# A two-layer trunk on one core: the attention's gate is summed in the first FFN, VectorE scales all columns of the handing over, and its first weight is split sooner

## The chip, the cores and the metric

The kernel runs on one core of a Trainium2 chip. The metric is the device time of one execution, in microseconds. Every kernel is also run once with the hardware profiler; that execution has its own time, and the times in the profile are counted from the start of its span.

## The reference

One sequence of 256 tokens with 2048 columns goes through two layers. Layer 0 is a causal pooling mixer and a SwiGLU FFN; then one latent key/value set is computed; layer 1 is latent attention over that set and a second FFN. Every sub-layer has its shift, scale and gate, which come from one vector `c`:

```python
sc = jax.nn.silu(c)
for i in range(DEPTH):                      # 2
    shift_m, scale_m, gate_m, shift_f, scale_f, gate_f = jnp.split(sc @ mod_w[i] + mod_b[i], N_MOD, axis=-1)
    if i == N_A:                            # layer 1: shared latent keys and values
        kv_shift, kv_scale = jnp.split(sc @ kv_mod_w + kv_mod_b, 2, axis=-1)
        h_kv = modulate(rmsnorm(x, kv_in_norm), kv_shift, kv_scale)
        kv = shared_kv(h_kv, w_dkv, kv_norm, w_uk, w_uv, w_kr, cos, sin)
    h = modulate(rmsnorm(x, norm_mix[i]), shift_m, scale_m)
    y = pool_mixer(h, pool_w[i], pool_scale[i]) if i < N_A else mla_mixer(h, kv, ...)
    x = x + gate_m[:, None, :] * y
    h = modulate(rmsnorm(x, norm_ffn[i]), shift_f, scale_f)
    x = x + gate_f[:, None, :] * swiglu(h, ffn_gate[i], ffn_up[i], ffn_down[i])
return rmsnorm(x, final_norm)
```

The FFN's inner width is 5632; there are 16 heads. All data are fp32.

## The kernel before

**Products.** Each fp32 weight tile of 1 MB (`raw`, 128 x 2048) is loaded by SyncE's queue (SP), and split into an upper half (ACT, L374) and a lower half (VectorE or DVE, L376), both `hl` tiles. The activations have two halves as well (`act` tiles), and a product is three: upper by upper, upper weight by lower activation, lower weight by upper activation (L398). A weight makes 24 products of 128x128 by 128x512 on TensorE (PE); the last third of them needs the lower weight. For the last weight of a sum the products go token block by token block (there are two, `tok` 0 and 1), so the lower weight is needed after 8 products there.

**The background.** The modulation vectors are products of one row with big matrices, and PE doesn't make them (but for the first ones): `Part.unit` loads one tile of 1 MB (L210) and sums it on DVE, one instruction over 128 x 2048 (L211, with a short reading of the accumulator). 168 such units stand in one list. Each split of a weight calls `tick()`, which adds `rate` to a credit and starts a unit when it reaches one; `plan(left, units)` first does what the plan before left over, and then sets the rate such that `left` units remain after so many ticks. `hold()` stops the units, `release(left, units)` goes on at a new rate. The loads share a ring of six `raw` tiles with the weights, and SP's queue issues both in program order. When all 16 units of a gate are summed, `spread` (L291 to L297) turns it on PE, copies it on ACT, writes it to DRAM from ACT's queue and broadcasts it into the one `gate` tile from GpSimd's (POOL).

**The stages**, by the profile: 0 to 190 us the pooling mixer; then the first FFN. It begins six of eleven chunks block by block as blocks of its input become ready (`start_ffn`, to about 389); in its last block round `todo` units are issued with the weights. `FFN_STEPS` then mixes projections (p), transpositions (t) and down projections (d); the last down projection (d3, 856 to 889) handles four column blocks (j = 0 to 3) of two weights each. Its results are gated and added (`piece`, L611 and L612); parts that are known before are added ahead (`known`, L604 and L605).

**The handing over** (889 to 917): the fourth column block's products aren't run by `ffn` but by `then_attention`, which is written out in the order in which each engine is to work (`manual_schedule`; elsewhere a scheduler sets it). It mixes the old products (`h.old`, L407) with the first products of the latent keys and values (a for the first weight, b for the second, 0 and 1 for the token block; each is three lists of four: [0] upper by upper, [1] lower weight, [2] lower activation). Between them stand the norm (L470, L472), the scaling of columns by it (`scale`, L476: DVE for column block 0, POOL for block 1), the transposition on PE (`turn`, L482), the shift and scale (`upper` on ACT, L490; `whole` on ACT, L499, or on DVE, L497) and the lower half (`lower`, DVE, L503). `split_upper` (ACT, L517) and `split_lower` (DVE, L520) split the two weights.

**After that** come the rest of the latent keys and values (to 936), the keys and values of the heads and the query latent (to 1012), the heads (to 1098: scores L1383 to L1386, softmax L1388 to L1401, transposition L1407, weights split in smaller pieces at L1362 and L1363), the output projection (to 1163), a second handing over with one column block, and the second FFN.

## Time and profile before

| | |
|---|---|
| median of 3 runs | 1918.96 us (1916.93 to 1919.68) |
| the profiled execution | 1918.19 us |
| its span | 1916.4 us |
| mean granted clock of TensorE | 0.987 |
| busy, share of the span: PE, DVE, ACT, POOL | 97%, 73%, 44%, 1% |
| background sums (L211): count, mean | 168, 2284 ns |
| lower splits (L376): count, mean | 289, 2289 ns |
| upper splits (L374): count, mean | 289, 1918 ns |
| DMA, mean over the span | 300 GB/s |

In rows of the profile, `L376 DVE TENSOR_TENSOR hl<-raw,hl 128x2048` is line 376 of the kernel, engine, operation, what it writes and reads, and its size. In the order of time a row has the start, the duration from the first to the last of `x` instructions in a row, and in brackets the idle time before it with what ended it. A row of windows has the window, its length and then for PE, PE's weight loads, DVE, ACT and POOL the busy time and the number of instructions, then the granted clock, the DMA engines' share and GB/s.

### The profile page before, as it was taken

How to read it: one execution, taken by the hardware profiler on the slowest of the kernel's cores; microseconds unless marked ns; L12 is line 12 of the kernel's file. 1: busy time of each engine (PE TensorE's matmuls, PEld its weight loads, DVE VectorE, ACT ScalarE, POOL GpSimd, SP SyncE). 2: the span in 40 equal slices, each digit the busy share in tenths (PEclk: the TensorE clock that was granted, in tenths of full speed). 3: DMA queues.
4: the chain of work that ended last, by engine and by line, in shares of the span. 5: the costliest groups of instructions: out<-in, count | busy, mean ns of one | idle time of the engine just before them, and what ended most of it. 6: DMA issues, size and time to landing. Idle time of an engine off the chain costs nothing.

```text
span 1916.4 us, 21930 instructions
## 1 busy us (share of the span) xinstructions
PE 1862.8 (97%) x8813; PEld 1507.8 (79%) x8813; DVE 1402.7 (73%) x1391; ACT 850.2 (44%) x958; POOL 26.9 (1%) x32
## 2 busy tenths in 40 slices
PE   7689999999999999999999999999999999999998
PEld 3255888888888888887889888888888888888887
DVE  2148799999788777799899966889785556645556
ACT  3125643444433334244678745634444433343343
POOL 0000000000000000002100000000000000000000
PEclk9789999999999999999999999999999999999999
DMA  9999998879998888897597775988776666665651
GB/s 399 398 418 417 368 364 333 319 299 361 357 344 332 327 330 326 332 373 274 212 371 291 293 278 194 397 318 335 260 284 240 241 240 239 249 222 205 220 198 44
DMA packets 86647, 574.98 MB, mean 300 GB/s; under 512 B 10977, under 2 KB 15505, under 8 KB 18321
## 3 DMA queue, kind: packets, MB, share of 16 engines
q1 hardware_dynamic: 86018, 570.42, 77.8%
q0 software_dynamic: 432, 3.15, 0.4%
q8 instruction: 69, 1.13, 0.2%
q14 instruction: 32, 0.26, 0.0%
q10 hardware_dynamic: 96, 0.02, 0.0%
HBM read 567.24 MB, written 6.32 MB: 299 GB/s over the span
## 4 chain that ended last, share of the span: by engine, by line
PE 69%; issue 22%; DMA 3%; DVE 3%; ACT 1%; SPq 0%; POOL 0%; POOLq 0%; DVEq 0%; ACTq 0%
PE ps L398 58%; DMA raw<-in_mod_w_dram 3%; PE ps L256 2%; PE ps L973 2%; PE ps L407 2%; PE ps L1288 2%; DVE raw L211 1%; PE ps L729 1%; PE ps L1197 1%; PE ps L540 0%; DMA raw<-in_mod_block_dram 0%; PE ps L196 0%; PE ps L948 0%; PE ps L770 0%; DVE hl L376 0%
## 5 line engine op out<-in xcount | busy, mean ns | idle before, releaser
L398 PE MATMUL ps<-hl,act 128*128 128x512 f32 x6744 | 1539.5, 390 | 1.9 <-DVE hl L376 1.0
L398 PEld LDWEIGHTS ps<-hl,act 128*128 128x128 f32 x6744 | 1263.0, 188 | 264.7 <-DVE hl L376 1.8
L376 DVE TENSOR_TENSOR hl<-raw,hl 128x2048 fp32r<-128x2048 f32 x289 | 661.1, 2289 | 253.2 <-ACT hl L374 252.5
L374 ACT ACTIVATE hl<-raw 128x2048 fp32r<-128x2048 f32 x289 | 553.1, 1918 | 647.8 <-PE ps L398 572.1
L211 DVE SCALAR_TENSOR_TENSOR raw<-raw,s_row 128x2048 f32<-128x2048 f32 x168 | 383.2, 2284 | 3.6 <-DMA raw<-in_mod_wt_dram 3.6
L256 PE MATMUL ps<-raw,s_strip 128*32 128x512 f32 x392 | 65.2, 760 | 34.6 <-DMA raw<-in_mod_w_dram 33.5
L698 DVE TENSOR_TENSOR act<-ps,act 128x512 f32<-128x512 f32 x96 | 64.5, 685 | 17.5 <-PE ps L398 17.5
L256 PEld LDWEIGHTS ps<-raw,s_strip 128*32 128x32 f32 x392 | 9.5, 121 | 70.0 <-DMA raw<-in_mod_w_dram 46.3
L784 DVE TENSOR_TENSOR x<-ps,x 128x512 f32<-128x512 f32 x32 | 22.1, 690 | 38.8 <-PE ps L398 38.8
L1288 PE MATMUL ps<-act,hl 128*128 128x256 f32 x384 | 49.6, 287 | 0.0
L1288 PEld LDWEIGHTS ps<-act,hl 128*128 128x128 f32 x384 | 48.3, 195 | 0.7 <-DVE act L1253 0.2
L407 PE MATMUL ps<-hl,act 128*128 128x512 f32 x192 | 47.0, 400 | 1.2 <-DVE act L503 1.2
L732 ACT ACTIVATE act<-ps 128x512 fp32r<-128x512 f32 x44 | 23.6, 594 | 50.0 <-PE ps L729 37.6
L407 PEld LDWEIGHTS ps<-hl,act 128*128 128x128 f32 x192 | 35.2, 188 | 10.7 <-ACT act L490 2.3
L263 DVE COPY t2k<-ps 128x256 f32<-128x256 f32 x4 | 1.7, 425 | 52.9 <-ACT t2k L262 52.9
L427 ACT ACTIVATE junk<-x 128x512 bf16<-128x512 f32 x23 | 14.5, 629 | 53.2 <-DVE x L612 37.6
L802 DVE TENSOR_TENSOR t2k<-ps,t2k 128x512 f32<-128x512 f32 x24 | 16.5, 689 | 28.5 <-PE ps L398 28.5
L798 ACT ACTIVATE t2k<-ps 128x512 f32<-128x512 f32 x24 | 14.2, 590 | 47.9 <-PE ps L398 47.9
L973 PEld LDWEIGHTS ps<-act,act 128*128 128x128 f32 x128 | 24.7, 200 | 11.6 <-issue 8.4
L696 ACT ACTIVATE act<-ps 128x512 f32<-128x512 f32 x32 | 19.1, 597 | 29.0 <-PE ps L398 28.8
L973 PE MATMUL ps<-act,act 128*128 128x256 f32 x128 | 31.9, 402 | 0.0
L733 DVE TENSOR_TENSOR act<-ps,act 128x512 fp32r<-128x512 f32 x44 | 28.1, 683 | 0.9 <-ACT act L732 0.9
(222 smaller groups left out, 911.6 us busy)
## 6 DMA issues: line engine op xcount, KB each, us to landing
raw<-in_mod_wt_dram SPq DMA_DIRECT2D x136, 1024.0 KB, 5.8
raw<-in_ffn_gate_dram SPq DMA_DIRECT2D x88, 1024.0 KB, 5.8
raw<-in_ffn_up_dram SPq DMA_DIRECT2D x88, 1024.0 KB, 5.1
raw<-in_ffn_down_dram SPq DMA_DIRECT2D x88, 1024.0 KB, 5.2
raw<-in_mod_w_dram SPq DMA_DIRECT2D x48, 1024.0 KB, 12.1
raw<-in_kv_mod_wt_dram SPq DMA_DIRECT2D x32, 1024.0 KB, 7.1
raw<-in_w_o_dram SPq DMA_DIRECT2D x16, 1024.0 KB, 6.1
raw<-in_mod_block_dram SPq DMA_DIRECT2D x8, 1024.0 KB, 12.5
```

Of the source, the lines that this page charges most:

```text
L211: dve.scalar_tensor_tensor(out=r, in0=r, scalar=1.0, in1=s_row, op0=ALU.mult, op1=ALU.mult, accum_out=self.sums[:, self.n:self.n + 1])
L256: pe.matmul(self.bank[m * STRIP:(m + 1) * STRIP, :], lhsT=weights(k), rhs=r[:, k, i, :], start=first, stop=last)
L374: hi_ins = act.activation(hi, r, AF.Copy)
L376: lo_ins = dve.tensor_tensor(out=lo, in0=r, in1=hi.bitcast(F32), op=ALU.subtract)
L398: pe.matmul(banks[tok], lhsT=t_[:, i, k, tok * P:(tok + 1) * P], rhs=w[:, k, :], start=first and n < len(part), stop=last and n >= len(ord ...
L407: pe.matmul(bank, lhsT=t_[:, i, k, tok * P:(tok + 1) * P], rhs=w[:, k, :], start=first and n == 0, stop=last and n == len(order) - 1)
L698: dve.tensor_tensor(out=part, in0=banks[tok], in1=part, op=ALU.add)
L732: act.activation(m[:, 0, :, ts_], v, AF.Copy)
L733: dve.tensor_tensor(out=m[:, 1, :, ts_], in0=v, in1=m[:, 0, :, ts_].bitcast(F32), op=ALU.subtract)
L784: dve.tensor_tensor(out=x[:, tok, js], in0=banks[tok], in1=x[:, tok, js], op=ALU.add)
L973: pe.matmul(mixed[g][:, n % 2, :], lhsT=wp[g][:, k, ns], rhs=pool_all[g // 2][:, g % 2, k, :], start=k == 0, stop=k == KL - 1)
L1288: pe.matmul(pt[:, h, :], lhsT=w(h0 + h, k), rhs=t_[:, i, k, :], start=n == 0, stop=n == 3 * KL - 1)
```

## The change

There are seven edits.

1. The plan of the background. The 16 units of the attention's gate (`n_mix`) no longer count among those that are left after the first FFN; `FFN0_UNITS` is 94 for 95, and `plan` and `hold`/`release` beside the query latent and the heads go. The first FFN after `start_ffn` now takes 89 units for 74 (91 in 94 ticks for 75 in 95), the keys and values 7 for 6, query latent and heads none for 19, the output projection 8 for 5. The second FFN keeps its 40. The gate's transposition and broadcast move from the heads into the keys and values.
2. `scale` runs on DVE for every column block; before, POOL did block 1.
3. In the last down projection `hold()` stands at column block 2, not 3.
4. `split_lower(w[0])` in the handing over stands ahead of the old products.
5. In `start_ffn`, block round 0, the eight units go with the third to the tenth of the twelve begun weights, not with the first eight. (In the first FFN the upper split of the second weight thereby comes to stand, on ACT, between the two halves of the four L1044, and three of that weight's products after the first four of the first weight's on PE.)
6. `run(a1[2], b0[2], ...)` for `run(b0[2], a1[2], ...)`.
7. `HEAD_UNITS` and `WO_LATE` have no use any more and go; `WO_UNITS` is 9 for 8.

```diff
--- before.py
+++ after.py
@@ -61,12 +61,11 @@
 BEGUN = 6
 ASIDE = 5
 
-FFN0_UNITS, MLA_UNITS, HEAD_UNITS, WO_UNITS, FFN1_UNITS = 95, 4, 16, 8, 60
+FFN0_UNITS, MLA_UNITS, WO_UNITS, FFN1_UNITS = 94, 4, 9, 60
 
 KNOWN = (1, 3, 5, 7, 9, 10, 11, 12)
 
-
-LATE, MLA_LATE, WO_LATE = 3, 5, 3
+LATE, MLA_LATE = 3, 5
 
 V_C, V_NM, V_NF, V_KVIN, V_KVN, V_QN, V_PS, V_B, V_KB, V_END = 0, 16, 48, 80, 96, 100, 104, 120, 312, 344
 
@@ -473,8 +472,8 @@
 
         def scale(self, tok, j):
             self.turned[tok, j] = t2k([P, CH]), ps_t().rearrange("p (k t) -> p k t", k=KL), t2k([P, KL, P])
-            (dve if j == 0 else pool).tensor_scalar(out=self.turned[tok, j][0], in0=x[:, tok, j * CH:(j + 1) * CH],
-                                                    scalar1=self.rstd[:, tok:tok + 1], scalar2=None, op0=ALU.mult)
+            dve.tensor_scalar(out=self.turned[tok, j][0], in0=x[:, tok, j * CH:(j + 1) * CH],
+                              scalar1=self.rstd[:, tok:tok + 1], scalar2=None, op0=ALU.mult)
 
         def turn(self, tok, j):
             xr, pt, _ = self.turned[tok, j]
@@ -745,7 +744,7 @@
             for j in range(ND):
                 js = slice(j * CH, (j + 1) * CH)
                 banks = [ps_t() for _ in range(NT)]
-                if last and j == ND - 1:
+                if last and j == ND - 2:
                     hold()
                 if last and j == ND - 1:
                     weights = [w_unit(wd[c, j]) for c in g]
@@ -884,7 +883,7 @@
                         begun[c][which].block(j, hT[j])
                     if n == 2 * len(begun) - 5:
                         pieces = ahead(j + 1)
-                    if todo:
+                    if todo and (j > 0 or n + 2 >= 2 * len(begun) - todo):
                         pump(1)
                         todo -= 1
                 pump(todo)
@@ -1107,9 +1106,9 @@
     for j in range(ND):
         sf_block(1, j, C_SF1, C_AF1)
     mod_part(1, 5, gate_to, "ffn1")
-    n_ffn1, n_blocks, n_mix = KD, KD // 2, KD
+    n_ffn1, n_blocks = KD, KD // 2
     n_late = n_ffn1 + LATE * n_blocks
-    n_all = n_ffn1 + ND * n_blocks + n_mix
+    n_all = n_ffn1 + ND * n_blocks
 
     hT, begun = start_ffn(0, first, hidden_T, lambda j, parts: halves_T(j, parts), ND - 1)
     plan(n_all + MLA_LATE, FFN0_UNITS)
@@ -1127,6 +1126,7 @@
         hkv, rstd = h.hT, h.rstd
         w = [w_load_of(dkv(j)) for j in range(2)]
         split_upper(w[0])
+        split_lower(w[0])
         run(h.old(0))
         h.start()
         h.piece(0)
@@ -1134,7 +1134,6 @@
         split_upper(w[1])
         h.scale(0, 0)
         h.scale(0, 1)
-        split_lower(w[0])
         fs = h.old(1)
         run(fs[:-KL])
         h.turn(0, 0)
@@ -1163,7 +1162,7 @@
         h.lower(0, 1)
         h.turn(1, 1)
         h.upper(1, 1)
-        run(b0[2], a1[2], b1[0], b1[1])
+        run(a1[2], b0[2], b1[0], b1[1])
         h.whole(1, 1, dve)
         h.lower(1, 1)
         run(b1[2])
@@ -1315,7 +1314,6 @@
     pool.memset(krT, 0.0)
     rope_end(kr_t, [(slice(0, ROPE), krT[0:ROPE, 0, :]), (slice(ROPE, P), krT[ROPE:P, 1, :])])
 
-    plan(n_all - n_mix - WO_LATE, HEAD_UNITS)
     cq = [ps_t() for _ in range(NT)]
     for j in range(ND):
         if len(hmx) < ND:
@@ -1430,11 +1428,9 @@
     pairs = H // HG
 
     act.activation(small([P, 1]), ones[:, 0:1], AF.Exp)
-    hold()
     heads = [project_heads(g) for g in range(2)]
     for o in heads:
         o.finish()
-    release(n_all - n_mix - WO_LATE, HEAD_UNITS - 8)
 
     w_o, ob = a["w_o"], []
```

In the changed kernel line numbers are one lower up to the keys and values, and two lower from the heads on.

How the instructions move on DVE, at three places. First the first FFN's last down projection, before: from the last transposition's lower half (L733) to the lower split of the second weight of column block 1 (`hl_5636`); L611 and L612 add results, L604 and L605 what is known.

```order
484 L733 TENSOR_TENSOR act_5487<-ps_5495,act_5487 128x4x128
485 L733 TENSOR_TENSOR act_5502<-ps_5503,act_5502 128x4x128
486 L733 TENSOR_TENSOR act_5502<-ps_5510,act_5502 128x4x128
487 L211 SCALAR_TENSOR_TENSOR raw_5522,sums_5279<-raw_5522,s_row 128x2048
488 L376 TENSOR_TENSOR hl_5559<-raw_5553,hl_5558 128x2048
489 L211 SCALAR_TENSOR_TENSOR raw_5555,sums_5279<-raw_5555,s_row 128x2048
490 L611 TENSOR_TENSOR x<-ps_5518,gate_3094 128x512
491 L376 TENSOR_TENSOR hl_5601<-raw_5598,hl_5600 128x2048
492 L611 TENSOR_TENSOR x<-ps_5519,gate_3094 128x512
493 L612 TENSOR_TENSOR x<-x,act_5205 128x512
494 L612 TENSOR_TENSOR x<-x,act_5206 128x512
495 L376 TENSOR_TENSOR hl_5636<-raw_5630,hl_5635 128x2048
```

The same place in the changed kernel. Ahead of these rows stand the lower split of the first weight of block 0, two L732 and one L210; the last row is the lower split of the second weight of block 1.

```order
505 L375 TENSOR_TENSOR hl_5610<-raw_5604,hl_5609 128x2048
506 L210 SCALAR_TENSOR_TENSOR raw_5606,sums_5360<-raw_5606,s_row 128x2048
507 L610 TENSOR_TENSOR x<-ps_5569,gate_2970 128x512
508 L603 TENSOR_TENSOR x<-x,gate_2970 128x512
509 L611 TENSOR_TENSOR x<-x,act_5249 128x512
510 L610 TENSOR_TENSOR x<-ps_5570,gate_2970 128x512
511 L375 TENSOR_TENSOR hl_5655<-raw_5649,hl_5654 128x2048
512 L611 TENSOR_TENSOR x<-x,act_5250 128x512
513 L604 TENSOR_TENSOR act_5249<-x,act_5249 128x512
514 L210 SCALAR_TENSOR_TENSOR raw_5651,sums_5360<-raw_5651,s_row 128x2048
515 L603 TENSOR_TENSOR x<-x,gate_2970 128x512
516 L375 TENSOR_TENSOR hl_5690<-raw_5684,hl_5689 128x2048
```

Two sums stand here where one did, L603 and L604 (the known parts) have moved ahead of the last split, and the two L732 of the ninth chunk stand further up.

Second the handing over, before: from the last sum to the second norm. L476 scales token block 0's first columns, L520 is the lower split of the first new weight.

```order
517 L211 SCALAR_TENSOR_TENSOR raw_5712,sums_5279<-raw_5712,s_row 128x2048
518 L465 TENSOR_REDUCE sm_5771<-ssq_5517 128x2
519 L466 TENSOR_SCALAR sm_5771<-sm_5771 128x2
520 L611 TENSOR_TENSOR x<-ps_5751,gate_3094 128x512
521 L612 TENSOR_TENSOR x<-x,act_5205 128x512
522 L470 SCALAR_TENSOR_TENSOR sm_5812<-ssq_5517,sm_5771 128x1
523 L476 TENSOR_SCALAR t2k_5816<-x,rstd_5772 128x512
524 L520 TENSOR_TENSOR hl_5776<-raw_5773,hl_5775 128x2048
525 L611 TENSOR_TENSOR x<-ps_5752,gate_3094 128x512
526 L612 TENSOR_TENSOR x<-x,act_5206 128x512
527 L503 TENSOR_TENSOR act_5769<-t2k_5818,act_5769 128x4x128
528 L470 SCALAR_TENSOR_TENSOR sm_5866<-ssq_5517,sm_5771 128x1
```

And now:

```order
535 L519 TENSOR_TENSOR hl_5824<-raw_5821,hl_5823 128x2048
536 L464 TENSOR_REDUCE sm_5819<-ssq_5568 128x2
537 L465 TENSOR_SCALAR sm_5819<-sm_5819 128x2
538 L610 TENSOR_TENSOR x<-ps_5799,gate_2970 128x512
539 L611 TENSOR_TENSOR x<-x,act_5249 128x512
540 L469 SCALAR_TENSOR_TENSOR sm_5861<-ssq_5568,sm_5819 128x1
541 L475 TENSOR_SCALAR t2k_5865<-x,rstd_5820 128x512
542 L475 TENSOR_SCALAR t2k_5869<-x,rstd_5820 128x512
543 L610 TENSOR_TENSOR x<-ps_5800,gate_2970 128x512
544 L611 TENSOR_TENSOR x<-x,act_5250 128x512
545 L502 TENSOR_TENSOR act_5817<-t2k_5867,act_5817 128x4x128
546 L469 SCALAR_TENSOR_TENSOR sm_5914<-ssq_5568,sm_5819 128x1
```

The sum is gone, the split (L519) is first, two scalings (L475) stand one behind the other, and the second token block's adds (L610, L611) follow them directly.

Third the heads, before: from a sum ahead of the first head's masked scores (L1390) to the second head's maximum (L1393). L1399 is a softmax's reciprocal, L849 to L852 the rotation of a query.

```order
619 L211 SCALAR_TENSOR_TENSOR raw_7150,sums_6588<-raw_7150,s_row 128x2048
620 L852 TENSOR_TENSOR act_6887<-t2k_6962 128x256
621 L1390 SCALAR_TENSOR_TENSOR t2k_7005<-ps_7000,con 128x128 x2
622 L211 SCALAR_TENSOR_TENSOR raw_7153,sums_6588<-raw_7153,s_row 128x2048
623 L1393 TENSOR_REDUCE sm_7009<-t2k_7005 128x3
624 L1390 SCALAR_TENSOR_TENSOR t2k_7024<-ps_7019,con 128x128
625 L1394 TENSOR_TENSOR sm_7009<-sm_7009 128x1
626 L1390 SCALAR_TENSOR_TENSOR t2k_7024<-ps_7019,con 128x128
627 L849 TENSOR_TENSOR t2k_7063<-t2k_7063,sin_t 128x256
628 L850 TENSOR_TENSOR t2k_7063<-t2k_7063,cos_t 128x256
629 L1399 RECIPROCAL sm_7015<-sm_7012 128x2
630 L1393 TENSOR_REDUCE sm_7028<-t2k_7024 128x3
```

And now, from the first head's masked scores to the second head's scaling by the reciprocal:

```order
632 L1388 SCALAR_TENSOR_TENSOR t2k_7040<-ps_7035,con 128x128 x2
633 L1388 SCALAR_TENSOR_TENSOR t2k_7059<-ps_7054,con 128x128
634 L1391 TENSOR_REDUCE sm_7044<-t2k_7040 128x3
635 L1388 SCALAR_TENSOR_TENSOR t2k_7059<-ps_7054,con 128x128
636 L1392 TENSOR_TENSOR sm_7044<-sm_7044 128x1
637 L1397 RECIPROCAL sm_7050<-sm_7047 128x2
638 L1391 TENSOR_REDUCE sm_7063<-t2k_7059 128x3
639 L1399 TENSOR_SCALAR t2k_7040<-t2k_7040,sm_7050 128x256
640 L1392 TENSOR_TENSOR sm_7063<-sm_7063 128x1
641 L849 TENSOR_TENSOR t2k_7095<-t2k_7095,cos_t 128x256
642 L1397 RECIPROCAL sm_7069<-sm_7066 128x2
643 L1399 TENSOR_SCALAR t2k_7059<-t2k_7059,sm_7069 128x256
```

The sums between are gone, and the second head's softmax ends ahead of the rotation's last steps.

## The prediction

> **What bounds the kernel now.** I read the page first, then a table of windows by stage, then the instructions in order of time wherever TensorE (PE) stands still. The rows give a window's length and then the busy time of each engine, the granted clock, the DMA engines' share and the rate.
>
> ```profile
> PE 1862.8 (97%) x8813; PEld 1507.8 (79%) x8813; DVE 1402.7 (73%) x1391; ACT 850.2 (44%) x958; POOL 26.9 (1%) x32
> 390.00:855.00 465.00, 465.00 (x2091) 385.82 (x2090) 377.77 (x296) 180.51 (x130) 0.70 (x1) 1.00 0.88 340
> 855.00:889.00 34.00, 33.85 (x154) 27.93 (x153) 33.97 (x36) 16.29 (x21) 0.00 (x0) 1.00 0.80 292
> 889.00:918.00 29.00, 25.61 (x117) 19.58 (x116) 24.16 (x33) 18.11 (x34) 15.28 (x8) 1.00 0.53 184
> 936.00:1012.00 76.00, 75.96 (x458) 67.24 (x457) 72.71 (x80) 56.50 (x92) 3.01 (x2) 1.00 0.92 352
> 1012.00:1098.00 86.00, 83.59 (x565) 77.22 (x565) 82.76 (x171) 69.58 (x183) 0.61 (x1) 0.98 0.78 286
> 1098.00:1163.00 65.00, 65.00 (x288) 53.79 (x288) 42.85 (x35) 27.40 (x25) 0.00 (x0) 1.00 0.72 270
> ```
>
> PE is the bound: 97% busy over the span. In the middle of the first FFN (390 to 855) it never stands still, so nothing done there can save anything; it can only cost. VectorE (DVE) has 465 - 377.8 = 87 us free there, but only 0.03 us in the FFN's last columns (855 to 889) and 3.2 us in the heads (1012 to 1098). PE loses 3.4 us in the handing over (889 to 918) and 2.4 us in the heads, where the clock is 0.98 as well. Those two places are what can be won: 5.8 us of 1918, and what the clock adds.
>
> **The sums moved into the first FFN.** Of the background's units, 74 ran in the FFN after its first blocks, 6 in the keys and values, 19 beside the query latent and the heads, 5 in the output projection; now 89, 7, none and 8. A unit is one load of 1 MB issued by SP and one sum on DVE.
>
> ```profile
> L376 DVE TENSOR_TENSOR hl<-raw,hl 128x2048 fp32r<-128x2048 f32 x121 | 276.5, 2288 | 60.4 <-ACT hl L374 60.1
> L211 DVE SCALAR_TENSOR_TENSOR raw<-raw,s_row 128x2048 f32<-128x2048 f32 x90 | 205.4, 2283 | 0.0
> 300.00:400.00 100.00, 100.00 (x447) 82.90 (x446) 91.07 (x84) 41.04 (x33) 0.00 (x0) 1.00 0.86 325
> 700.00:800.00 100.00, 100.00 (x451) 83.05 (x450) 78.06 (x62) 38.81 (x25) 0.00 (x0) 1.00 0.83 317
> SPq L210 <- DVE hl L376: 175.8, 56, 9.2
> 809.93 1.92 ACT L374 ACTIVATE hl<-raw 128x2048 fp32r<-128x2048 f32 x1 [0.58 <-DMA raw<-in_ffn_gate_dram]
> 814.92 1.92 ACT L374 ACTIVATE hl<-raw 128x2048 fp32r<-128x2048 f32 x1 [3.06 <-DMA raw<-in_ffn_gate_dram]
> 819.91 1.92 ACT L374 ACTIVATE hl<-raw 128x2048 fp32r<-128x2048 f32 x1 [3.07 <-DMA raw<-in_ffn_gate_dram]
> 856.02 32.92 PE L398 MATMUL ps<-hl,act 128*128 128x512 f32 x144
> ```
>
> The last row gives a weight's time on PE: the next product starts at 888.78, so 32.76 / 144 x 24 = 5.46 us. The plan goes from 75 units in 95 weights to 91 in 94, from 0.79 to 0.97 a weight. DVE then has 2.29 + 0.97 x 2.28 = 4.50 us a weight, and the additions. The 15 more sums are 34 us out of the 87 us free. SP's queue gets 15 more loads ahead of weights, 1.97 transfers a weight. At 810 to 820, after a refill from empty, a weight and a unit between them land every 4.99 us, which is 0.47 us less than PE takes. Elsewhere SP waits for buffers (the row of SP: 56 times, 175.8 us), not the buffers for transfers. So I put the middle at **0** (bounds 0 and -1.5, from the few places just after a refill, where little lead is left).
>
> **The FFN's last columns.** DVE has no time free here, and the order now puts more ahead of the splits.
>
> ```profile
> 855.47 2.47 DVE L733 TENSOR_TENSOR act<-ps,act 128x512 fp32r<-128x512 f32 x4
> 869.11 2.28 DVE L376 TENSOR_TENSOR hl<-raw,hl 128x2048 fp32r<-128x2048 f32 x1
> ```
>
> From 855.47 to the end of the second column's second split at 871.32 DVE did 15.85 us of work. PE began the columns at 856.02 and needs that lower half after three weights and 8 of the next one's products, 856.02 + 16.38 + 1.82 = 874.2: 2.9 us of cover. In the new order the same stretch holds seven long instructions (2.21 us from start to start), two of L733 and seven additions (0.60 each): 15.5 + 1.2 + 4.2 = 20.9 us. That is 5.0 us more against 2.9 us of cover, a stall of 2.1 us; a later split is late by another 0.1 or 0.2. Nothing issues units in the last two columns, so it ends there. **-2.3 us** (bounds 0, if DVE enters the stretch with a lead, and -4, if the additions also meet a wait for PE).
>
> **The start of the first FFN.** Eight units begin two blocks later, so ACT's order changes: the second weight's upper half is now split between the two halves of L1044.
>
> ```profile
> 168.74 2.08 ACT L1044 ACTIVATE act<-t2k,cols 128x256 fp32r<-128x256 f32 x4 [1.42 <-DVE cols L897]
> 170.72 1.90 ACT L374 ACTIVATE hl<-raw 128x2048 fp32r<-128x2048 f32 x1
> 169.39 14.06 PE L398 MATMUL ps<-hl,act 128*128 128x512 f32 x60 [0.95 <-ACT act L1044]
> 183.83 5.51 PE L398 MATMUL ps<-hl,act 128*128 128x512 f32 x23 [0.38 <-DVE hl L376]
> 189.92 1.43 PE L398 MATMUL ps<-hl,act 128*128 128x512 f32 x5 [0.58 <-DVE hl L376]
> ```
>
> Two waits for DVE, which was behind a sum each time, go: 0.38 + 0.58 = 1.0 us, 1.25 us by the starts of the products. PE does four products (to 170.3) and then needs the weight that ACT splits from about 169.8 to 171.7: 1.4 us lost. **-0.2 us** (bounds -1.4 and +1.2). The second FFN's start has no such pressure: 0.
>
> **The handing over.** Four edits act here together: no sum stands ahead of the last column's adds, the first lower split is made before, DVE does all four scalings, and two lists of products change places.
>
> ```profile
> 894.28 2.29 DVE L211 SCALAR_TENSOR_TENSOR raw<-raw,s_row 128x2048 f32<-128x2048 f32 x1
> 899.87 0.49 DVE L476 TENSOR_SCALAR t2k<-x,rstd 128x512 f32<-128x512 f32 x1 [0.69 <-POOL rstd L472]
> 900.27 2.29 DVE L520 TENSOR_TENSOR hl<-raw,hl 128x2048 fp32r<-128x2048 f32 x1
> 899.93 3.98 POOL L476 TENSOR_SCALAR t2k<-x,rstd 128x512 f32<-128x512 f32 x1
> 900.41 0.66 PE L482 MATMUL ps<-con,t2k 128*128 128x128 f32 x4 [1.41 <-DVE t2k L476]
> 903.97 0.66 PE L482 MATMUL ps<-con,t2k 128*128 128x128 f32 x4 [0.80 <-POOL t2k L476]
> 912.88 0.96 PE L407 MATMUL ps<-hl,act 128*128 128x512 f32 x3 [1.18 <-DVE act L503]
> ```
>
> The first wait (1.41) goes, but barely: counted from the start of the old products (888.78), and with DVE late by the stall above, the row of adds and the split that now stands ahead end at 7.7 us and the scaling at 10.0, where PE comes to L482 after 44 products, at 10.0. Before, the scaling ended at 11.6. The second (0.80) is POOL's 3.98 us for a piece that DVE does in 0.49 us: it goes. The third (1.18) is b0[2] for the second of two L503; now a1[2] goes first, which needs the first of them, and is late by about 0.5. I lay the new order out with these durations: the DVE rows now in front of the second column's split are two scalings (0.98) where there was one, so b0[1] waits some 0.6, and a0[2] 0.6 for L503. By the starts of the products the three old waits are 1.57 + 1.08 + 1.34 = 4.0 us; new ones are 1.7 us, and about 0.7 us of ACT's pacing goes with the idle time. **+3.0 us** (bounds +1.0, if each new wait is doubled, and +4.0). POOL's four scalings at L528 begin sooner, when PE does not yet wait for them: 0.
>
> **Keys and values, query latent.** The gate's transposition and its broadcast (one product, one ACT copy, two DMAs, one of them on POOL's queue) move in from the heads, and thirteen sums become seven. PE stands still 0.04 us of 76, and by the starts of its products it is 1.5 us late in all. I take **+0.3 us** of that (bounds -0.5 and +1).
>
> **The heads.** Until nearly their end no sum stands between DVE's small instructions.
>
> ```profile
> 1018.94 2.29 DVE L211 SCALAR_TENSOR_TENSOR raw<-raw,s_row 128x2048 f32<-128x2048 f32 x1
> 1021.89 2.28 DVE L211 SCALAR_TENSOR_TENSOR raw<-raw,s_row 128x2048 f32<-128x2048 f32 x1
> 1024.10 0.55 DVE L1393 TENSOR_REDUCE sm<-t2k 128x3 f32<-128x384 f32 x1
> 1030.35 0.41 ACT L1400 ACTIVATE t2k<-t2k,sm 128x128 f32<-128x128 f32 x1
> 1030.81 0.55 PE L1407 MATMUL ps<-con,t2k 128*128 128x128 f32 x3 [1.97 <-ACT t2k L1400]
> 1011.59 3.04 PE L1288 MATMUL ps<-act,hl 128*128 128x256 f32 x24
> 1033.33 3.81 PE L1288 MATMUL ps<-act,hl 128*128 128x256 f32 x24
> ```
>
> The second head's transposition waits 1.97 us for ACT's L1400. ACT is late because the first maximum (L1393) stood behind the sum at 1021.89 until 1024.10. Without it the maximum comes at about 1022.0, both softmaxes end near 1026.5, and PE wants them at 1028.4: that wait goes, with 1.9 us in hand. Behind it the clock falls: 24 products of L1288 take 3.81 instead of 3.04 us, and eight products before them lose 0.7 us, together 1.5 us. The Trainium skill's "TensorE: Matmul & The Clock Gate" (Part 1, What's actually happening) lets the clock fall only after an idle window of about 3.4 us; by that rule the 1.97 us would have cost no clock, and this term would be 1.5 us smaller. The rows at 1030.81 and 1033.33 show otherwise, and the measurement decides. So 2.41 us idle and 1.5 us of clock are at stake; **+3.9 us** (bounds +2.0, if a wait for ACT remains, and +5.0, with the delays too short to show as idle time).
>
> **The output projection.** Three more units: 6.9 us on DVE, which is busy 42.85 of 65: 0.
>
> **The sum**: -0.2 + 0 - 2.3 + 3.0 + 0.3 + 3.9 = 4.7 us less. The profiled execution took 1918.19 us (span 1916.4), which gives 1913.5. The median of the runs shown is 0.77 us above that, and they lie 2.75 us apart; I give **1913.6**.
>
> **The rivals.** *DVE's lag in the FFN eats it.* The FFN's last columns cost 4 and the places after a refill 1.5, the rest as forecast: 1918.2 - 1.0 = 1917.2. For it: 0.03 us free in 855 to 889. Against: 87 us free before. *No stall there.* DVE enters with a lead of 2 us: 1911.2. For it: the first split of the columns is already in hand when they begin. *The heads do not gain*, because ACT (69.6 of 86 us) sets the pace in place of DVE: only 2 us, 1915.4, with the stall in full 1917. Against: ACT has idle time before 1023. That the sums stay in the heads is excluded by the order. *Slower: the transfers become the bound in the first FFN.* With 1.97 transfers a weight, PE waits once a transfer takes over 5.46 / 1.97 = 2.77 us, 378 GB/s. The rows of 300 to 400 and 700 to 800, scaled to a full share, give 325 / 0.86 = 378 and 317 / 0.83 = 382 GB/s, just at that point. Against: 2.5 us each at 810 to 820, which is 420 GB/s. At 2.9 us a weight would be short by 0.25 us, 23 us in 94 weights; some 9 us of lead (the longest wait of SP) go first, 14 us stay: 1913.5 + 14 = 1927. It comes out slower from 2.87 us on. The Trainium skill's "DMA: Bandwidth & Descriptors" (Specifications) has about 358 GB/s as the limit of HBM for one core: as an estimate 2.93 us a transfer, and 1933. The spacing at 810 to 820 does not agree with it here.
>
> **How the numbers follow.** Forecast 0.50, lag 0.20, no stall 0.12, heads 0.10, slower 0.08. The bounds of the forecast's terms reach from 1909 to 1920 where not all fall the same way, and this holds the first four cases; the slower one is left out: **1909.0 to 1920.5**. A measurement here tells about 0.2% (3.8 us) from no change: faster is below 1915.1, slower above 1922.8. Faster: most of the forecast (0.44), no stall (0.12), a little of the heads (0.03): 0.59. Slower: 0.08, and 0.01 of the lag. The same: 0.32.
>
> **What would show it.** In the new profile: PE without a wait at L482 in the handing over; no wait at L1407 over 0.5 us and a clock of 1.00 in the heads; a wait of 1 to 2 us of PE for the lower splits in the first FFN's last columns, and one for ACT at its start. PE idle in the middle of the first FFN, with ACT's splits waiting for DMA, would mean the slower case. A wait of PE for POOL at the following latent columns, or for the gate's broadcast, would be a step I have missed.

## The result, and the profile after

| | before | after |
|---|---|---|
| median | 1918.96 us (1916.93 to 1919.68) | 1933.11 us (1931.36 to 1934.79) |
| ratio | | 1.0074, interval 1.0060 to 1.0087 |
| span of the profiled execution | 1916.4 us | 1931.3 us |
| mean granted clock | 0.987 | 0.983 |

The change makes the kernel 14 us slower. 4.7 us less were forecast. The time lies outside the range, and its sign is that of a rival to which 0.08 was given, at a time (1927) and by a mechanism that are not the measured ones.

The windows of the changed kernel by stage (length, then busy time of PE, PE's weight loads, DVE, ACT and POOL, granted clock, DMA share, GB/s), at the places that answer to those shown of before:

```profile
PE 1870.2 (97%) x8813; PEld 1511.0 (78%) x8813; DVE 1406.3 (73%) x1393; ACT 849.8 (44%) x958; POOL 19.0 (1%) x30
390.00:855.00 465.00, 462.52 (x2074) 381.38 (x2073) 406.12 (x326) 180.24 (x129) 0.70 (x1) 1.00 0.93 369
855.00:900.00 45.00, 42.83 (x191) 34.58 (x190) 43.99 (x42) 20.70 (x21) 0.00 (x0) 1.00 0.92 337
900.00:930.00 30.00, 28.63 (x132) 21.85 (x131) 22.19 (x37) 19.41 (x40) 9.24 (x6) 1.00 0.40 146
948.00:1024.00 76.00, 71.31 (x409) 63.24 (x408) 54.35 (x58) 51.42 (x81) 1.72 (x3) 0.96 0.74 276
1024.00:1110.00 86.00, 82.67 (x563) 76.52 (x562) 64.59 (x152) 69.41 (x183) 0.00 (x0) 0.98 0.48 171
```

DVE did get its free time: 21 us in the heads (64.6 busy of 86, 82.8 before), 22 in the keys and values. PE did not use it. It stands still 4.7 us in the keys and values, where it had lost 0.04, 2.5 in the FFN's middle, where it had lost nothing, and 3.3 in the heads, where it was 2.4. What PE waits for, over the whole span (total, times, longest, in us; the first row is the mixer's wait for its loads, 33.5 before):

```profile
PE ps L255 <- DMA raw<-in_mod_w_dram: 34.0, 17, 9.6
PE ps L291 <- DVE cols L299: 4.7, 1, 4.7
PE ps L397 <- ACT hl L373: 3.5, 8, 0.8
PE ps L1405 <- ACT t2k L1398: 3.3, 3, 2.0
...
PE ps L397 <- DVE hl L375: 1.0, 1, 1.0
PE ps L397 <- ACT act L1043: 1.0, 1, 1.0
PE ps L406 <- DVE hl L519: 0.9, 1, 0.9
```

L291 is the transposition of a gate. The table adds up what PE loses in each stage. It is worked out from the starts of all its products: every start-to-start time above the usual one of that form, so a halved clock counts too.

| PE's loss, us | before | after | forecast | measured |
|---|---|---|---|---|
| first 20 us of the first FFN | 1.8 | 3.3 | +0.2 | +1.5 |
| from there to its last columns | 2.7 | 7.6 | 0 | +4.9 |
| last columns | 0.1 | 2.6 | +2.3 | +2.4 |
| handing over | 5.3 | 2.7 | -3.0 | -2.5 |
| keys and values, query latent | 1.4 | 8.3 | -0.3 | +6.9 |
| heads | 5.3 | 6.1 | -3.9 | +0.8 |
| all after the mixer | 21.8 | 35.8 | -4.7 | +14.0 |

The other 0.9 us of the spans' difference lie in the pooling mixer, whose length went from 167.6 to 171.0 us through all profiled executions, whatever was changed.

**Keys and values.** The changed kernel in order of time, all engines (start, duration, engine, line and operation; in brackets the idle time before):

```profile
956.95 5.92 PE L1287 MATMUL ps<-act,hl 128*128 128x256 f32 x48
...
961.32 2.29 DVE L210 SCALAR_TENSOR_TENSOR raw<-raw,s_row 128x2048 f32<-128x2048 f32 x1
...
962.70 5.63 PE L397 MATMUL ps<-hl,act 128*128 128x512 f32 x24
...
967.95 2.28 DVE L210 SCALAR_TENSOR_TENSOR raw<-raw,s_row 128x2048 f32<-128x2048 f32 x1
...
970.16 2.28 DVE L210 SCALAR_TENSOR_TENSOR raw<-raw,s_row 128x2048 f32<-128x2048 f32 x1
...
972.71 0.16 DVE L299 TENSOR_TENSOR cols<-sums,vcol 128x16 f32<-128x16 f32 x1
...
973.02 0.37 PE L291 MATMUL ps<-con,cols 128*16 128x128 f32 x1 [4.69 <-DVE cols L299]
```

The last of the attention gate's sums end at 972.4, its columns (L299) come at 972.7, and PE has been standing at the gate's transposition since 968.3. All else that it could do stands behind that one small product in its fixed order. Then the clock is down: the next 48 products of L1287 take 8.29 us (973.14 to 981.43), where such 48 had taken 5.92.

**The FFN's middle.** The changed kernel in order of time at the first of six waits (the row of SPq is the issue of a load):

```profile
472.33 0.33 SPq L386 DMA_DIRECT2D raw<-in_ffn_down_dram  x1
473.10 1.92 ACT L373 ACTIVATE hl<-raw 128x2048 fp32r<-128x2048 f32 x1 [0.40 <-DMA raw<-in_ffn_down_dram]
...
484.64 0.60 ACT L781 ACTIVATE x<-ps 128x512 f32<-128x512 f32 x1 [9.62 <-PE ps L397]
485.14 1.91 ACT L373 ACTIVATE hl<-raw 128x2048 fp32r<-128x2048 f32 x1
...
487.08 2.29 DVE L375 TENSOR_TENSOR hl<-raw,hl 128x2048 fp32r<-128x2048 f32 x1 [3.73 <-ACT hl L373]
...
487.10 3.26 PE L397 MATMUL ps<-hl,act 128*128 128x512 f32 x13 [0.45 <-ACT hl L373]
```

The weight that ACT splits at 485.14 was asked for at 472.33, and the trace has its landing at 480.2. ACT had nothing to do from 475.0 to 484.6. But its next instruction was the copy of a bank (L781) that PE was still filling, and the split stands behind it. When the copy begins, PE has products for 2.0 us more (to 486.65); the copy and the split take 2.4.

The other five waits have the same form in the trace. Each split begins directly behind a copy (once L781, four times L797) for which ACT had waited 2.5 to 11.0 us, and its weight had landed 1.3 to 8.5 us before. With the product behind each, which is slow by 0.11 us, the six make 4.1 of the 4.9 us.

**The heads.** The changed kernel in order of time near their end:

```profile
1086.37 1.89 ACT L373 ACTIVATE hl<-raw 128x2048 fp32r<-128x2048 f32 x1
...
1088.17 0.39 ACT L1398 ACTIVATE t2k<-t2k,sm 128x128 f32<-128x128 f32 x1
1088.29 2.29 DVE L375 TENSOR_TENSOR hl<-raw,hl 128x2048 fp32r<-128x2048 f32 x1 [0.67 <-ACT hl L373]
...
1090.50 0.16 DVE L1397 RECIPROCAL sm<-sm 128x2 f32<-128x2 f32 x1
1090.69 0.40 ACT L1398 ACTIVATE t2k<-t2k,sm 128x128 f32<-128x128 f32 x1
...
1091.15 1.12 PE L1405 MATMUL ps<-con,t2k 128*128 128x128 f32 x3 [2.00 <-ACT t2k L1398]
```

The wait is the one of before, 2.0 us for a softmax's last step. What delays the softmax is now the split of an output projection's weight, 1.9 us on ACT and 2.3 us on DVE. The second head's transposition, which waited at 1030 us before, waits no more, as forecast; two waits have come in at 1080 and 1091.

### The profile page after: what moved, and what is told of

The parts are those of the page before. It is cut to its first block, busy times and chain, and to the rows that moved or that the text cites. A ratio compares the mean times of both kernels' runs of the same rounds, so it can differ in the third digit from the quotient of the medians.

```text
span 1931.3 us, 21989 instructions
## 1 busy us (share of the span) xinstructions
PE 1870.2 (97%) x8813; PEld 1511.0 (78%) x8813; DVE 1406.3 (73%) x1393; ACT 849.8 (44%) x958; POOL 19.0 (1%) x30
## 4 chain that ended last, share of the span: by engine, by line
PE 89%; DMA 4%; DVE 4%; ACT 2%; issue 1%; SPq 0%; POOL 0%; POOLq 0%; DVEq 0%; ACTq 0%
PE ps L397 76%; DMA raw<-in_mod_w_dram 3%; PE ps L255 2%; PE ps L972 2%; PE ps L406 2%; PE ps L1287 1%; DVE raw L210 1%; DVE hl L375 1%; PE ps L728 1%; ACT hl L373 1%; PE ps L1196 1%; PE ps L539 0%; DMA raw<-in_mod_block_dram 0%; PE ps L195 0%; PE ps L947 0%
## 5 line engine op out<-in xcount | busy, mean ns | idle before, releaser
L375 DVE TENSOR_TENSOR hl<-raw,hl 128x2048 fp32r<-128x2048 f32 x289 | 660.7, 2288 | 250.4 <-ACT hl L373 250.2
L210 DVE SCALAR_TENSOR_TENSOR raw<-raw,s_row 128x2048 f32<-128x2048 f32 x168 | 383.1, 2284 | 1.6 <-DMA raw<-in_mod_wt_dram 1.6
L1287 PE MATMUL ps<-act,hl 128*128 128x256 f32 x384 | 51.2, 292 | 0.0
L1287 PEld LDWEIGHTS ps<-act,hl 128*128 128x128 f32 x384 | 49.7, 200 | 0.7 <-DVE act L1252 0.2
L797 ACT ACTIVATE t2k<-ps 128x512 f32<-128x512 f32 x24 | 14.2, 590 | 56.4 <-PE ps L397 56.4
L426 ACT ACTIVATE junk<-x 128x512 bf16<-128x512 f32 x23 | 14.5, 631 | 54.6 <-DVE x L611 38.7
L972 PEld LDWEIGHTS ps<-act,act 128*128 128x128 f32 x128 | 24.8, 200 | 11.7 <-issue 8.4
L732 DVE TENSOR_TENSOR act<-ps,act 128x512 fp32r<-128x512 f32 x44 | 28.3, 682 | 0.7 <-ACT act L731 0.6
## 6 DMA issues: line engine op xcount, KB each, us to landing
raw<-in_mod_w_dram SPq DMA_DIRECT2D x48, 1024.0 KB, 11.7
```

What stands on the lines that cost most here:

```text
L210: dve.scalar_tensor_tensor(out=r, in0=r, scalar=1.0, in1=s_row, op0=ALU.mult, op1=ALU.mult, accum_out=self.sums[:, self.n:self.n + 1])
L375: lo_ins = dve.tensor_tensor(out=lo, in0=r, in1=hi.bitcast(F32), op=ALU.subtract)
L732: dve.tensor_tensor(out=m[:, 1, :, ts_], in0=v, in1=m[:, 0, :, ts_].bitcast(F32), op=ALU.subtract)
L972: pe.matmul(mixed[g][:, n % 2, :], lhsT=wp[g][:, k, ns], rhs=pool_all[g // 2][:, g % 2, k, :], start=k == 0, stop=k == KL - 1)
L1287: pe.matmul(pt[:, h, :], lhsT=w(h0 + h, k), rhs=t_[:, i, k, :], start=n == 0, stop=n == 3 * KL - 1)
```

## The experiments

In all, "before" is the kernel before, run again on the same chip; its medians lay between 1917.88 and 1919.28 us. The losses of PE are those of the table's kind. The changed kernel was timed only for the result, so a difference from it is uncertain by the 1.4 us by which the medians of before differ.

**The sums alone** (the plan of edit 1, nothing else):

```diff
-FFN0_UNITS, MLA_UNITS, HEAD_UNITS, WO_UNITS, FFN1_UNITS = 95, 4, 16, 8, 60
+FFN0_UNITS, MLA_UNITS, WO_UNITS, FFN1_UNITS = 94, 4, 9, 60
-    n_ffn1, n_blocks, n_mix = KD, KD // 2, KD
+    n_ffn1, n_blocks = KD, KD // 2
...
-    plan(n_all - n_mix - WO_LATE, HEAD_UNITS)
-    hold()
-    release(n_all - n_mix - WO_LATE, HEAD_UNITS - 8)
```

> The new plan of the background alone; the handing over and the FFN's start as before. Theory (the moved sums pile up): PE loses 4.3 us in the middle of the first FFN, 2 to 3 in its last columns, 6 at the gate's transposition in the keys and values, and wins nothing in the heads: 1931 to 1934 us. Rival (the four edits of the handing over or the FFN's start carry the loss): 1918 to 1924 us.

Measured: 1933.15 us, 1.0077 (1.0060 to 1.0093). The theory's time; the loss is that of the plan of sums. The parts are others than expected: the middle 5.9 us and the last columns 2.9 more than before, the handing over 2.6 more (PE waits 3.2 us for a lower split there), the keys and values only 1.5 and the heads 1.1.

**The handing over alone** (edits 2, 3, 4 and 6):

```diff
-            (dve if j == 0 else pool).tensor_scalar(out=self.turned[tok, j][0], ...
+            dve.tensor_scalar(out=self.turned[tok, j][0], ...
-                if last and j == ND - 1:
+                if last and j == ND - 2:
                     hold()
         split_upper(w[0])
+        split_lower(w[0])
         run(h.old(0))
...
-        split_lower(w[0])
-        run(b0[2], a1[2], b1[0], b1[1])
+        run(a1[2], b0[2], b1[0], b1[1])
```

> The edits of the handing over alone (all scalings on DVE, first split sooner, hold a column sooner, the two lists swapped), sums where they were. Theory: the three waits of PE there (4.0 us by the starts of the products) shrink to about 1.5 and no stall comes in the FFN's last columns, since no more sums are there: 1915.5 to 1917.5 us. Rival (the stall in the last columns comes from the edits themselves): 1918 to 1920 us, with PE waiting over 1 us for a lower split between 856 and 889.

Measured: 1919.02 us, 1.0003 (0.9994 to 1.0013), no difference. The handing over gives its 2.6 us (5.3 to 2.7), and no stall comes in the last columns (0.1), as the theory has it. But the keys and values lose 2.7 us: the earlier hold leaves two sums over, and 15 run there in place of 13.

**The start alone** (edit 5):

```diff
-                    if todo:
+                    if todo and (j > 0 or n + 2 >= 2 * len(begun) - todo):
                         pump(1)
```

> The later units at the FFN's start alone. Theory: PE waits for ACT's split of the second weight at about 170 us and its clock stays at half for some 6 us after it, as in the changed kernel: 1.3 to 2 us slower, 1920.3 to 1921 us. Rival (the half clock came from elsewhere): within 0.5 us of before.

Measured: 1918.64 us against 1917.88, 1.0006 (0.9997 to 1.0015), which can't be told from no change. In the profile the loss of PE in the first 20 us goes from 1.8 to 3.5, as in the changed kernel: PE waits 0.2 us for ACT's split, and the granted clock is 0.55 from 171 to 178 us. But that clock is no sign of this edit. Profiles of kernels that issue the units at the start as before have it too: 0.54 from 169 to 176 us in the version that beats both, 0.53 with three things put right (both below). Among all profiles only that of the kernel before is free of it. So the wait for the split is shown, and that the edit costs clock is not.

**The gate's transposition later** (the changed kernel, `deferred` is put to `pending` and flushed once the query latent stands):

```diff
-            pending.append((0, spread))
+            (deferred if name == "mla" else pending).append((0, spread))
...
     kv.append(keys_values(H // KG - 1, query_latent))
+    pending.extend(deferred)
+    flush()
```

> The changed kernel with the attention gate's transposition put off until the query latent is done. Theory: PE's wait of 4.7 us for the gate's columns and the half clock behind it (some 6 us in all) go: 1926 to 1928 us. Rival (the weights behind it are late as well, as VectorE's seven sums stand in one row): another wait takes its place, 1930 to 1933 us.

Measured: 1927.82 us, 1.0049 (1.0034 to 1.0064), 5.3 less than the changed kernel. The loss in the keys and values falls from 8.3 to 3.0 us. The wait for L299 is gone, and so is the half clock behind it; from 945 to 1030 us PE has one wait left, of the rival's kind:

```profile
PE ps L539 <- ACT t2k L529: 1.7, 1, 1.7
```

**The hold later** (the changed kernel, `hold()` at column block 3 again):

```diff
-                if last and j == ND - 2:
+                if last and j == ND - 1:
                     hold()
```

> The changed kernel with the hold one column later, as before. Theory (the hold pushes two sums ahead of the gate's columns in the keys and values, and PE waits for those): 4 to 5 us less there, 2 to 4 us more in the FFN's last columns and the handing over: 1931 to 1933 us. Rival (the gate is late whatever the hold does): no gain there, 1935 to 1937 us.

Measured: 1930.83 us, 1.0070 (1.0055 to 1.0084), 2.3 us less than the changed kernel. The waits of PE from the handing over to the query latent:

```profile
PE ps L406 <- DVE hl L375: 3.2, 1, 3.2
PE ps L291 <- DVE cols L299: 1.7, 1, 1.7
PE ps L406 <- DVE hl L519: 0.9, 1, 0.9
```

The gate's wait is 1.7 for 4.7 us, and the handing over loses 5.0 us more (7.8 for 2.7). So the hold's two sums are paid in either place, and with the earlier hold the gate is waited for longer. PE's loss after the mixer is the same in both profiles to 0.1 us, and this one's mixer is 1.9 us shorter: that the later hold saves the 2.3 us is not shown.

**Half the sums' work.** The changed kernel; in the first FFN after its first blocks (there `thin[0]` is true) the sum covers half the tile and leaves the other half out:

```diff
-            dve.scalar_tensor_tensor(out=r, in0=r, scalar=1.0, in1=s_row, ...
+            n_ = D // 2 if thin[0] else D
+            dve.scalar_tensor_tensor(out=r[:, :n_], in0=r[:, :n_], scalar=1.0, in1=s_row[:, :n_], ...
```

> The changed kernel, but between the first blocks and the end of the first FFN a unit's sum covers half of its columns (the other half is left out of the result); the loads are whole. VectorE has some 1.1 us less a unit, the transfers are the same. Theory (the six raw tiles come free too late, since a weight's load waits until VectorE has done the sum ahead): the waits of PE for ACT's splits in the middle, 5 us in the changed kernel, and the stall of 2.4 us in the last columns go; under 1 us is left in both. Rival (the transfers are the bound): 4 to 5 us stay in the middle.

Measured: 1928.56 us in one run. DVE is busy 329 us of 473 in the middle, and PE's loss there, counted from 390 us on, is 7.0 us, exactly as with the whole sums. The waits of PE for ACT's splits there, in the changed kernel and in this one (whose lines are three higher):

```profile
PE ps L397 <- ACT hl L373: 2.5, 6, 0.5
PE ps L400 <- ACT hl L376: 2.5, 6, 0.5
```

DVE's work is not what PE waits for in the middle. In the last columns it is a part: 1.2 for 2.6 us.

**Half the loads**, summed twice, and then **half of both** (again in that stretch alone):

```diff
...
+                sync.dma_start(r[:, :D // 2], rows[:, :D // 2])
+                for _ in range(2):
+                    dve.scalar_tensor_tensor(out=r[:, :D // 2], in0=r[:, :D // 2], ...
```

```diff
+            n_ = D // 2 if thin[0] else D
+            sync.dma_start(r[:, :n_], self.w[...][:, :n_])
```

> The changed kernel, but in the same stretch a unit loads only half of its columns and VectorE sums that half twice (the other half is left out of the result): half the unit's transfer, slightly more time on VectorE (2 x 1.2 for 2.3 us). Theory (VectorE frees the tiles too late): 3 to 6 us of PE's waits stay in the middle. Rival (the transfers are the bound): under 1 us is left there.

> The changed kernel; in the first FFN after its first blocks a unit loads and sums only half of its columns (the other half is left out of the result). Theory (the transfers are the bound in the middle, since halving the sums alone left its 7.0 us as they were): that falls to 2 to 3 us, as before the change. Rival (the order of the instructions, which is the changed kernel's in all of these, makes the waits): about 7 us stay.

Measured: 1950.48 and 1943.19 us, one run each, with 29.8 and 18.9 us lost in the middle. Neither decides anything here. The waits became waits for DVE, and DVE waited for the half loads (in the second 82.7 us in 40 times for one tensor's alone): the scheduler put the sums elsewhere in DVE's order, and the sums hold up the splits behind them. They say nothing on the rate of the transfers.

**Fourteen units without a load**, and **seven raw tiles**, again on the changed kernel:

```diff
+            count[0] += thin[0]
+            empty = thin[0] and count[0] % 6 == 0
+            if not empty:
+                sync.dma_start(r, ...)
-            dve.scalar_tensor_tensor(out=r, in0=r, ...
+            dve.scalar_tensor_tensor(out=r, in0=s_row if empty else r, ...
```

```diff
-        return work.tile(shape, dt, tag="raw", bufs=6, name=nm("raw"))
+        return work.tile(shape, dt, tag="raw", bufs=7, name=nm("raw"))
-        return work.tile(shape, dt, tag="t2k", bufs=7, name=nm("t2k"))
+        return work.tile(shape, dt, tag="t2k", bufs=5, name=nm("t2k"))
```

> The changed kernel; of the units between the first blocks and the end of the first FFN every sixth (14 in all) has no load and sums a tile that is already there (those 14 tiles are left out of the result). Data as before the change, VectorE's work and the ring's places as after it. Theory (too many transfers for the stretch): PE's loss in the middle falls from 7.0 to 2 to 3 us. Rival (the ring's places, whatever they carry): 5 to 7 us stay.

> The changed kernel with seven raw tiles for six (the 2 KB tiles are five for seven, to make room; that can cost elsewhere, so the middle of the first FFN alone is read). Theory (too many transfers): 5 to 7 us stay there, somewhat later. Rival (the ring's places): 2 to 4 us.

Measured: 1935.91 us in one run, with 11.7 us lost in the middle, where DVE's order had changed again (five waits for L375 that are not in the changed kernel); and 1934.67 us in one run, with 6.9 us. The first is inconclusive. The second is telling in an unexpected way: one more tile leaves the waits not "somewhat later" but where they were. Counted from the start of the span all six come 2.1 us earlier than in the changed kernel, as its mixer was 2.1 us shorter, and they are as long to the hundredth (0.61 us by the starts, the second 0.39). Half the sums' work shows the same six, and so do the sums alone, with a seventh at 815 us. A wait for data would have moved; the landings in the trace of the changed kernel say the same. This led to ACT's order.

**The copies on DVE** (the changed kernel):

```diff
-                        act.activation(x[:, tok, js], banks[tok], AF.Copy)
+                        dve.tensor_copy(x[:, tok, js], banks[tok])
```

> The changed kernel with the first down projection's results copied out by VectorE, not by ACT (the copies at L781). ACT's order is otherwise the same. Theory (ACT's fixed order: a weight's split stands behind the copy of a bank that PE is still filling, though the weight has long landed): the two waits of PE at 486 and 505 us go, those at 527, 638, 683 and 838, whose split stands behind L797, stay. Rival (the weights land late): all six stay.

Measured: 1927.5 us in the one run. PE of this kernel around the places in question (its mixer is 2.0 us shorter):

```profile
469.76 20.35 PE L397 MATMUL ps<-hl,act 128*128 128x512 f32 x89
489.95 1.04 PE L728 MATMUL ps<-con,t2k 128*128 128x128 f32 x8
490.74 5.70 PE L397 MATMUL ps<-hl,act 128*128 128x512 f32 x24
496.28 1.03 PE L728 MATMUL ps<-con,t2k 128*128 128x128 f32 x8
497.07 27.46 PE L397 MATMUL ps<-hl,act 128*128 128x512 f32 x120
524.98 5.32 PE L397 MATMUL ps<-hl,act 128*128 128x512 f32 x22 [0.45 <-ACT hl L373]
```

The waits at 486 and 505 are gone, the one at 527 (here 525) stays, and so do the three later ones. That is the theory's result and can't be the rival's. The loss in the middle falls by 0.7 us, as a new small wait comes at 813; the rest of the 5.6 us by which this one run is faster lies in the mixer, the keys and values and the heads, and nothing is made of it.

**Three things put right** (the changed kernel with the later transposition, the units at the start as before and the copies on DVE):

> The changed kernel with three things put right: the gate's transposition after the query latent, the units at the FFN's start as before, the copies of L781 on VectorE. Theory (the causes are separate and add up): 1933.1 - 5.3 - 1.4 - 1.1 = 1925.3 us, 1924 to 1926.5. Rival (one gives way to the other): 1927 to 1930 us.

Measured: 1925.01 us, 1.0039 (1.0025 to 1.0053), which is 0.3 us from the theory's sum, in part by luck. In the profile, whose time is this median, the keys and values lose 4.9 us less than in the changed kernel (5.3 were expected) and the middle 0.7 less (1.1). The start gives 0.4 of its 1.4 us, since its clock is at half again. The rest was made up elsewhere: the heads lose 1.3 us less, because the clock does not fall behind their wait of 2.0 us, and the mixer is 0.7 us shorter.

**Half of the sums moved** (the kernel before, `n_mix = KD // 2`):

```diff
-    n_ffn1, n_blocks, n_mix = KD, KD // 2, KD
+    n_ffn1, n_blocks, n_mix = KD, KD // 2, KD // 2
```

> The kernel before with 8 of the gate's 16 sums moved to the first FFN (82 units there, 0.88 a weight in place of 0.79 and 0.97), 8 left beside the heads. Theory (a lack of VectorE's lead, which sets in between these rates): PE waits under 1.5 us in the FFN's middle, no gate to wait for in the keys and values, 1917 to 1920 us. Rival (each sum moved costs the same, 15 us for 15): 1925 to 1927 us.

Measured: 1922.0 us, 1.0016 (1.0006 to 1.0025), 2.7 us for eight sums, between the two theories and nearer to the first. Only one wait for ACT's split is left in the middle (0.5 us), and the keys and values are as before (1.4). The theory's name for the cause (DVE's lead) was wrong, as the halved sums show. Another cost shows: a wait of 2.6 us for a lower split in the handing over.

**The output projection's splits later** (the changed kernel; behind the last softmax, then behind the last but two; `ends` collects the last two instructions of each softmax):

```diff
...
-        hi, lo = w_unit(w_o[u, 0])
+        with tc.issue_after(ends[-1][0].ins), tc.issue_after(ends[-1][1].ins):
+            hi, lo = w_unit(w_o[u, 0])
```

> The changed kernel with the splits of the output projection's first column block held behind the last softmax on ACT and VectorE. Theory (in the heads those splits, 1.9 and 2.2 us each, stand between the softmaxes' steps in the place of the sums): PE's two waits of 1.2 and 2.0 us for L1398 go and the clock with them, 3 to 5 us are won in the heads and 1 to 3 lost at the start of the output projection: 1930 to 1932 us. Rival (the softmax chain itself is too long for PE): the waits at L1405 stay.

> The changed kernel with the output projection's first splits held only behind the last but two softmaxes. Theory (splits among the softmaxes' steps make PE's waits at the end of the heads): no wait at L1405 or its like before the last pair, 2 to 4 us less in the heads, part of it given back in the output projection. Rival: the waits move to the last pair, the sum stays at 6 us.

Measured: 1938.19 us, 1.0098 (1.0081 to 1.0115), and 1930.66 us in one run with `ends[-3]`. All waits of PE from 1020 to 1130 us in the first of them (total, times, longest):

```profile
PE ps L397 <- ACT hl L373: 5.4, 1, 5.4
PE ps L1414 <- ACT t2k L1409: 2.1, 1, 2.1
```

The second has there only the second of these rows. In both the waits of the transposition for L1398 (3.3 us in all) are gone, so the splits among the softmaxes do cause them. In their place comes one of 2.1 us at the weighting of the values, and in the first one of 5.4 us for a split that was held too long. The time of the first misses its forecast by 6 us, and the heads of the second lose 4.6 for 6.1 us.

**A version that beats both** (the kernel before with the four edits of the handing over, and the plan stretched so that the keys and values get 13 sums again):

```diff
-FFN0_UNITS, MLA_UNITS, HEAD_UNITS, WO_UNITS, FFN1_UNITS = 95, 4, 16, 8, 60
+FFN0_UNITS, MLA_UNITS, HEAD_UNITS, WO_UNITS, FFN1_UNITS = 92, 4, 16, 8, 60
```

> The edits of the handing over alone, on the kernel before, with the plan stretched so that the units which the earlier hold stops are done in the first FFN (rate 0.82 in place of 0.79) and the keys and values get 13 sums as before, not 15. Theory (the hold pushed two sums into the keys and values, and these cost the 2.7 us lost there in the run of the edits alone): 2 to 3 us less than before, 1915.5 to 1917 us by a median of before of 1918.5. Rival (the wait at the heads' end grows with any new order): within 1 us of before.

Measured: 1915.72 us against 1918.54, 0.9988 (0.9979 to 0.9997), 2.8 us less. The windows of the handing over, the keys and values and the heads:

```profile
891.00:917.00 26.00, 24.88 (x113) 19.22 (x112) 19.27 (x33) 16.27 (x35) 9.24 (x6) 1.00 0.35 122
937.00:1011.00 74.00, 73.95 (x442) 65.30 (x441) 70.72 (x77) 54.93 (x87) 3.01 (x2) 1.00 0.95 361
1011.00:1091.00 80.00, 77.60 (x544) 72.17 (x543) 78.08 (x168) 66.92 (x181) 0.61 (x1) 1.00 0.78 280
```

PE stands still 1.1 us in the handing over and 0.05 in the keys and values. In this profile the handing over loses 2.6 us less than before. The heads keep their 2.4 us of idle time, but the clock does not fall there (1.4 us less); at the first FFN's start it does fall, as it did not before (1.1 us more), and the FFN's middle loses 1.2 us more, 0.7 of them in one new wait for ACT's split at 724 us. Both differences of the clock are, by the last section, chance. So the time fits the handing over's 2.6 us, and the rest of it can't be told part by part.

**Both together** (that version, with the output projection's splits behind the last but two softmaxes):

> The edits of the handing over with the stretched plan, and the output projection's first splits behind the last but two softmaxes. Theory (as at the changed kernel, where this took 1.8 us): 1914 to 1915.5 us. Rival (with sums beside the heads the splits are late for the projection): 1916 to 1919 us.

Measured: 1916.73 us against 1917.9, 0.9991 (0.9982 to 1.0001): no gain from the later splits, as the rival has it.

## Why the prediction was wrong

**The keys and values: the step that failed most.** The prediction counted the gate's transposition as "one product, one ACT copy, two DMAs" that "move in from the heads", and gave the stage +0.3 us. It priced the instruction and did not ask when its input is ready. The gate's last seven sums run in that stage; the transposition stands in PE's order ahead of 48 products, and costs a wait of 4.7 us and 2.4 us of clock. The run with the transposition put off shows this cost as 5.3 us of time. The prediction's last paragraph had named a "step I have missed" for "the gate's broadcast", without a price. It also held edit 3 for a gain alone; a held unit is not saved but done later, here right in front of the gate.

**The FFN's middle: "0 (bounds 0 and -1.5)", measured -4.9.** The cover was worked out for DMA (5.0 us of transfer to 5.46 us of PE a weight) and DVE (4.5 us). Both held: half of DVE's work changed nothing, and the loads had landed. What failed is that an engine's cover was taken as a rate. ACT is 39% busy there, and the term has no line on its order; but its instructions are in a fixed order, and the scheduler had put more weights' splits right behind a copy that waits for PE: nine of them from 390 to 865 us, and PE waits for six, where before there were six and PE waited for none. That the copy in front is the cause is shown for the two waits of L781 by the run that moves these copies; for the four at L797 it rests on the trace (the order on ACT and the landings) and was not tried by a run.

**The heads: +3.9 forecast, -0.8 measured.** The diagnosis of before was right in its place: the transposition at 1030 us no longer waits. The step "that wait goes" ended there, and what is late next was looked for only to the second head. ACT's rows of the output projection's splits among the softmaxes were in the order of the changed kernel, and were not laid out to the heads' end. Two waits of 1.2 and 2.0 us, the second with the clock's fall, took the place of the one. That fall is chance: in four other profiles with the same wait it is missing, and the heads lose 1.3 us less there. The rival "the heads do not gain, because ACT sets the pace" had the outcome roughly, and 0.10.

**The start: -0.2 forecast, -1.5 measured, 0.1 outside its bound of -1.4.** PE's wait for ACT's split was seen, and its size as well: where the first four products ran at full speed (the run with the later transposition, for one) it costs 1.2 us by the starts, for 1.4 forecast. In the changed kernel these products ran at half speed, so that PE came later to the split and stood still for 0.2 us only. The clock was left out of this term, and it fell there with and without edit 5 (the rows stand in the last section). Where it falls, the two waits for DVE are gone without the edit too, so the edit has nothing to win. Among profiles with the same stretch of half clock, those with edit 5 lose 0.3 to 1.3 us more than those without it; how much of the 1.5 us is chance stays open.

**Right in size:** the last columns, 2.4 us lost for 2.3. The mechanism is there in part: one of the two waits is for DVE's lower split (1.0 us); the other is for ACT's upper split (0.8 us), which stood behind a square of L426 that waited for DVE's late additions. Halving the sums takes 1.4 of the 2.4 us away. **Right too:** the handing over, +2.5 for +3.0; the waits at L482 are gone, and of the forecast new ones those for the second weight's lower split (0.9 us) and for L502 (0.3) are there. **The slower rival** (transfers become the bound) has no support: the middle moved 369 GB/s at a share of 0.93, and the seventh tile and the halved sums left every wait in its place. That the prediction's estimate of 1933 us for this rival meets the measured time is chance. That the data's amount itself plays no part could not be shown, since the runs with fewer transfers changed DVE's order.

**A slip in the rivals' sums.** With 4 us lost in the last columns and 1.5 in the middle the terms add up to 1.5 us less, that is 1916.7, where the rival of DVE's lag has 1917.2. Either counts as the same by the prediction's limits.

## What to carry to other kernels

Free time on an engine is no cover by itself: engines work in a fixed order, so ask of each instruction that the next stage needs what stands directly in front of it and what that waits for, above all a copy of a result in front of the preparation of the next input. When work is moved or held, follow it to where it lands, and find what its last result is waited for by. Waits that keep their length and their place when data and buffers are changed are waits of order, and an experiment that moves the one instruction in front shows it sooner than any on rates. A difference in the clock between two profiles is put down to an edit only when further profiles, with the edit and without it, agree.
